# One layer's MLP recast in two phases, with its inner rows parked in DRAM and its second product done by seven block products

## The chip, the cores and the metric

The kernel runs on one core of a Trainium2 chip. A core has TensorE (PE in the profile, its weight load PEld), VectorE (DVE), ScalarE (ACT), GpSimd (POOL), and SyncE (SP), whose queue issues nearly all DMAs. TensorE writes to PSUM, which VectorE and ScalarE read; weights, activations and operands lie in SBUF. The metric is the device time of one execution in microseconds (us): the kernel before takes 1152.82 us, the median of three runs (1152.68 to 1153.12).

## The reference, cut to what matters

There are 512 latent and 256 context tokens (768 together) of width 1024, and two layers. Layer 0 mixes by pooling, layer 1 by attention, and each ends in a squared-ReLU MLP with inner width 4096. Before and after each part rows are normalised, scaled and shifted by vectors that come from a conditioning vector through `w_ada` (six slabs of 1024 columns a layer: shift, scale and gate for the mixer, then for the MLP).

```python
def sq_relu_mlp(h, w_in, w_out):
    return jnp.square(jax.nn.relu(h @ w_in)) @ w_out

# layer 0, latent and context tokens alike
m = sq_relu_mlp(modulate(rms_norm(x, g_mlp_pre), sh2, sc2), w_mlp_in, w_mlp_out)
x = x + gt2 * rms_norm(m, g_mlp_post)
```

Everything is float32. The kernel splits each operand into a high part in TensorE's rounded 32-bit type and a low part, the rest, and forms a product as three: high by high, high by low, low by high.

## The kernel before, in words

The change lies in the MLP of layer 0 (`mlp0`). Its inner width of 4096 is cut into 16 groups of 256 (`NG`), two blocks of 128 rows each. A group has two products. The first, `h @ w_in`, gives the group's inner rows (256 by 768 tokens). Groups 0 and 1 do it plainly (`Inner`). Groups 2 to 15 do it by a Strassen-Winograd scheme with seven block products (`Seven`): the 1024 of the contraction are halved, so are the tokens and the 256 inner rows, and seven products of half blocks, 12 matmuls of 384 columns each (`chain`), stand for eight. The sums of activation blocks are made once (`sums`), those of the weight blocks for every group (`weights_sums`): VectorE makes them, ScalarE rounds the high parts, VectorE subtracts for the low parts. Within a group the chains share four accumulators `a`, `b`, `c` and `e` in PSUM: chain 2 adds to `a` behind ScalarE's copy of `a` to `b`, chain 4 behind a copy of `a` to `c`, and chain 6 behind VectorE's reading of `a`.

ScalarE then takes ReLU and square, high and low parts go to SBUF (`hids0`), and the second product, `out_mm`, multiplies them by the group's 256 rows of `w_mlp_out`: for each of six tiles of 128 tokens and each half of 512 output columns 6 matmuls of 512 columns, 72 in a group. The result of each is added to `acc` in SBUF, mostly by VectorE (`out_ev`), in part by seeding the PSUM bank from `acc` through ScalarE and copying it back. The last two groups are done tile by tile in `finish`, where the normalisation that follows the MLP, and layer 1's query, key and value projections, run alongside.

Each group also works at the conditioning slabs that are needed later (`ada_step` in `mid0` and `extra0`): VectorE forms them in `ada_sum`, column by column of the contraction, for three slabs with both conditioning vectors (`dual`) and three with one (`lone`), and four small matmuls in `ada_fin` lay a slab down. In the stage before the MLP other slabs are formed by TensorE instead: `ada_mm` runs four float32 matmuls of a 128 by 32 stationary block on 512 columns for one loaded unit, each on its own 32 columns of the array, `ada_turn` transposes the result on VectorE, and `ada_sel` sums the pieces with small matmuls.

Raw weights pass through a pool of three buffers of 1 MB (`rawp`); SP issues the loads in order, and a load waits until its buffer is free. `work` tiles (`tmp`) come from a pool of three too. PSUM has two double tiles (`psA`, four banks) and four single ones (`psB`). The order on the engines is made by a planner that simulates the program with its own costs, within the dependences; in the stage before the MLP the code gives times by hand (`st.at`). The residual rows `xr` are parked in DRAM (`spill`) before the sums take their place in SBUF, and come back in `before0`.

## Time and profile before

| What | Value |
|---|---|
| median of three runs | 1152.82 us |
| profiled execution, first to last instruction (span) | 1150.8 us |
| what lies around the span, against the median | 2.0 us |
| PE, PEld busy | 1129.7 us (98%), 976.6 us (85%) |
| DVE, ACT, POOL busy | 925.9 us (80%), 640.0 us (56%), 76.0 us (7%) |
| traffic to and from DRAM | 154.20 MB, mean 134 GB/s |
| layer-0 MLP on TensorE, from group 1 to the end of the second product | 95.4 to about 586 us |

The profile holds one execution. A line of the groups gives engine and operation, the tiles written and read, shapes and count, then busy time, the mean of one instruction, and the idle time before them with what ended it. Nearly all instructions carry one line number, L68, since a helper records them; they are told apart by tiles: `psin` is the first product, `pso` the second, `psada` a conditioning slab on TensorE, `rows` one on VectorE, `units` and `rb` hold split weights and inner rows, `raw` a loaded weight, `acc` the running output. Matmul records overlap, so the time that one matmul really takes is read from start to start and not from its duration.

### The profile page before, as it was taken

How to read it: one execution, taken by the hardware profiler on the slowest of the kernel's cores; microseconds unless marked ns; L12 is line 12 of the kernel's file. 1: busy time of each engine (PE TensorE's matmuls, PEld its weight loads, DVE VectorE, ACT ScalarE, POOL GpSimd, SP SyncE). 2: the span in 40 equal slices, each digit the busy share in tenths (PEclk: the TensorE clock that was granted, in tenths of full speed). 3: DMA queues.
4: the chain of work that ended last, by engine and by line, in shares of the span. 5: the costliest groups of instructions: out<-in, count | busy, mean ns of one | idle time of the engine just before them, and what ended most of it. 6: DMA issues, size and time to landing. Idle time of an engine off the chain costs nothing. (4 is left out here: it accounts for less than half of the span.)

```text
span 1150.8 us, 15601 instructions
## 1 busy us (share of the span) xinstructions
PE 1129.7 (98%) x5998; PEld 976.6 (85%) x5998; DVE 925.9 (80%) x1539; ACT 640.0 (56%) x1142; POOL 76.0 (7%) x82
## 2 busy tenths in 40 slices
PE   6999999999999999999999999999999999999998
PEld 5579889998899988999878889988988888888886
DVE  5798488889889898897578688977887779778875
ACT  6476655554345434555795368863876436435534
POOL 3040000000000000000241312100000000000000
PEclk9999999999999999999999999999999999999999
DMA  9993233244434434344642200046244224224304
GB/s 352 399 391 105 74 110 110 80 140 147 144 113 147 146 130 146 128 143 145 227 145 104 98 1 19 17 144 225 75 146 147 78 69 146 81 66 147 110 17 149
DMA packets 100042, 154.20 MB, mean 134 GB/s; under 512 B 7120, under 2 KB 72448, under 8 KB 99968
## 3 DMA queue, kind: packets, MB, share of 16 engines
q1 hardware_dynamic: 99872, 153.19, 39.2%
q8 instruction: 47, 0.77, 0.3%
q14 instruction: 27, 0.22, 0.1%
q10 hardware_dynamic: 96, 0.02, 0.0%
HBM read 143.75 MB, written 9.45 MB: 133 GB/s over the span
## 5 line engine op out<-in xcount | busy, mean ns | idle before, releaser
L68 PE MATMUL pso<-units,rb 128*128 128x512 f32 x1152 | 277.7, 392 | 0.0
L68 PEld LDWEIGHTS pso<-units,rb 128*128 128x128 f32 x1152 | 214.8, 188 | 41.4
L68 DVE TENSOR_TENSOR acc<-acc,pso 128x512 f32<-128x512 f32 x192 | 128.3, 683 | 63.7 <-PE pso L68 63.6
L68 DVE SCALAR_TENSOR_TENSOR rows<-raw,cond,rows 128x256 f32<-128x256 f32 x280 | 122.2, 482 | 0.9
L68 PE MATMUL psin<-ra 128*128 128x512 f32 (+1 forms) x424 | 112.3, 369 | 0.6 <-ACT work L68 0.6
L68 PE MATMUL psin<-ra,rb 128*128 128x512 f32 (+1 forms) x384 | 101.6, 360 | 0.1
L68 DVE TENSOR_TENSOR units<-raw,units 128x1024 fp32r<-128x1024 f32 (+2 forms) x69 | 83.1, 1214 | 15.9 <-ACT units L68 15.8
L68 ACT CAST units<-raw 128x1024 fp32r<-128x1024 f32 (+2 forms) x71 | 70.8, 1019 | 41.6 <-PE pso L68 20.8
L68 PE MATMUL psin<-rb,ra 128*128 128x384 f32 (+1 forms) x324 | 90.6, 356 | 0.0
L68 PEld LDWEIGHTS psin<-ra 128*128 128x128 f32 x424 | 77.8, 188 | 12.1 <-ACT work L68 1.0
L68 PE MATMUL psin<-ra,units 128*128 128x384 f32 x432 | 82.5, 336 | 0.0
L68 PE MATMUL pso<-units,pairs 128*128 128x512 f32 x336 | 82.3, 389 | 0.0
L68 ACT ACTIVATE work<-psin 128x512 f32<-128x512 f32 (+3 forms) x66 | 36.1, 552 | 82.8 <-PE psin L68 75.1
L68 PEld LDWEIGHTS psin<-ra,units 128*128 128x128 f32 x432 | 76.5, 188 | 2.8
L68 PEld LDWEIGHTS psin<-ra,rb 128*128 128x128 f32 x384 | 66.7, 189 | 11.7 <-issue 0.9
L68 PEld LDWEIGHTS pso<-units,pairs 128*128 128x128 f32 x336 | 63.1, 188 | 13.1
L68 PE MATMUL psin<-sums,units 128*128 128x384 f32 x336 | 63.8, 336 | 0.0
L68 PEld LDWEIGHTS psin<-rb,ra 128*128 128x128 f32 x324 | 58.6, 188 | 5.4
L68 ACT COPY acc<-pso 128x512 f32<-128x512 f32 x68 | 38.6, 592 | 40.3 <-PE pso L68 40.2
L68 PEld LDWEIGHTS psin<-sums,units 128*128 128x128 f32 x336 | 59.1, 188 | 1.3
L68 ACT ACTIVATE work<-work 128x768 f32<-128x768 f32 (+1 forms) x50 | 41.4, 831 | 32.2 <-DVE work L68 31.7
L68 ACT CAST rb<-raw 128x2048 fp32r<-128x2048 f32 (+2 forms) x18 | 25.8, 1432 | 59.2 <-PE pso L68 55.9
(221 smaller groups left out, 2096.6 us busy)
## 6 DMA issues: line engine op xcount, KB each, us to landing
raw<-in_w_ada SPq DMA_DIRECT2D x48, 1024.0 KB, 5.4
raw<-in_w_mlp_in SPq DMA_DIRECT2D x32, 1024.0 KB, 5.3
raw<-in_w_mlp_out SPq DMA_DIRECT2D x32, 1024.0 KB, 5.7
raw<-in_w_qkv SPq DMA_DIRECT2D x6, 1024.0 KB, 5.1
spill<-xl SPq DMA_DIRECT2D x8, 512.0 KB, 10.8
xl<-spill SPq DMA_DIRECT2D x8, 512.0 KB, 10.9
raw<-in_w_o SPq DMA_DIRECT2D x4, 1024.0 KB, 5.0
xl<-in_x SPq DMA_DIRECT2D x4, 512.0 KB, 5.7
```

The costliest lines, as they stand in the source:

```text
L68: z = made(*args, **kw)
```

## The change

Layer 0's MLP is done in two phases. In the first, all groups form their inner rows; the squared rows go to a DRAM buffer `hidden` (float32, 32 blocks of 128 by 768) by SP's queue, and no second product stands between the groups. The split weights of successive groups alternate between two homes, and their accumulators between `psA` and `psB`. In the second phase the inner rows come back. Groups 0 to 11, as three stretches of 1024 of the contraction, are multiplied with `w_mlp_out` by seven block products each: tokens, contraction and output columns are halved, `prep` makes the sums and splits of a product two products ahead, `product_tile` runs 12 matmuls of 512 columns for each of three token tiles, and the results gather in seven blocks `M`, which `joins` combines in the third stretch. Groups 12 and 13 follow as plain products (24 matmuls for each of six tiles), and groups 14 and 15 in `finish` as before.

The three `dual` slabs move from VectorE to TensorE (`ada_dot`, `ada_end`): each is two halves of two units, set behind chain 3 and chain 5 of even groups 4 to 10, and within groups 1 and 2. The three `lone` slabs stay on VectorE. The residual rows are parked in DRAM earlier (`row_away`). The core of the diff:

```diff
+    def after(z, a):
+        if a is not None:
+            tc.add_manual_dep(z.ins, a.ins.name, ISSUE, reason="row order")
...
+    def ada_mm(i, m, c0, width, u, behind=None):
...
-                pin(te.matmul(ps[q:q + 32, :], cond[:, k, :], raw[:, kk, 512 * h:512 * h + 512],
-                              start=(u == 0), stop=(k >= KT - nk), skip_group_check=True), m in (GT1, SC2, SH2))
+                z = te.matmul(ps[q:q + 32, :], cond[:, k, :], raw[:, kk, 512 * h:512 * h + 512],
+                              start=(u == 0), stop=(k >= KT - nk), skip_group_check=True)
+                pin(z, m in (GT1, SC2, SH2))
+                after(z, behind)
...
+        if zeroed:
+            ve.memset(ps[:, 0:2 * n], 0.0)
...
+            if self.hid is None:
+                sy.dma_start(hidden[:, 2 * self.g + f], r)
+                return
...
-        B11, B21 = put(unit[1][:, 0:2048], rv[:, 0], 1024)
+        home = unit[2 - g % 2]
+        B11, B21 = put(home[:, 0:2048], rv[:, 0], 1024)
...
+            if g % 2 == 0:
+                hi, lo = (z.rearrange("p (m k n) -> p m k n", m=3, n=P)[:, m0:m0 + nm] for z in (rb[:, 0:1536], rb[:, 1536:3072]))
+            else:
...
+        def run(self, between=None, turns={}):
+            g = self.g
+            if g % 2:
+                a, e, b, c = (psB.tile([P, 512], F32, tag="b", name="psin")[:, 0:HN] for _ in range(4))
+            else:
+                px, py = (psA.tile([P, 2, 512], F32, tag="a", name="psin") for _ in range(2))
+                a, b, c, e = px[:, 0, 0:HN], px[:, 1, 0:HN], py[:, 0, 0:HN], py[:, 1, 0:HN]
+            if g == NG - 1:
+                r0, r1 = (work_tile()[:, 0:TOK] for _ in range(2))
+            else:
+                r0, r1 = (acc[:, TOK * z:TOK * z + TOK] for z in (2 * (g % 2), 2 * (g % 2) + 1))
+            if g == 3:
+                for z in (b, c):
+                    te.matmul(z, self.products[0][0][0][0], A11[0][0], start=True, stop=True)
...
+            if 3 in turns:
+                turns[3](self.ends[3])
...
+            if 5 in turns:
+                turns[5](self.ends[5])
...
-            hi, lo = self.hid
-            for f, r in enumerate((r0, r1)):
+            for f, r in ((1, r1), (0, r0)):
                 sc.activation(r, r, AF.Square)
-                sc.copy(hi[:, f, :], r)
-                ve.tensor_tensor(out=lo[:, f, :], in0=r, in1=hi[:, f, :], op=ALU.subtract)
+                sy.dma_start(hidden[:, 2 * g + f], r)
...
+    def row_away(t):
+        tc.keep_in_program_order(sy.dma_start(spill[:, t], xr[:, t]))
+
+    for t in (1, 2, 0, 3, 4, 5):
+        st.at(75.3 if t < 5 else 79.2, row_away, t)
...
-        wo_ = w_out(0, 0, one(unit[2]), True)
+        products = weights_sums(2)
+        halves = list(dual)
+        for u in range(2):
+            ada_load(*halves[0], 512, u)
         sums()
-        for g in range(NG - 1):
-            if g:
-                wo_, products = w_out(0, g, one(unit[2])), weights_sums(g + 1)
-            part = (g, inner.hid, wo_)
+        pinned[0] = False
+        inner = Inner(1, wi, aH, aL, None, chunks0, TOK)
+        inner.part(0, 0)
+        ada_dot(*halves[0], inner.last)
+        inner.part(0, 1, range(4))
+        ada_end(*halves[0], inner.last)
+        inner.part(0, 1, range(4, KT))
+        ada_dot(*halves[1], inner.last)
+        for f in range(2):
+            inner.square(f)
+        late_ = ExitStack()
+        NC = 3
+        W = [rb[:, 0:4096], unit[0], unit[1]]
+        regions = [(0, 0), (1, 0), (1, 1), (0, 1)]
+        xat = [n % 4 for n in range(7 * NC)]
+        xat[-3:] = [3, 0, 2]
...
+        def put(hi, lo, src):
+            sc.copy(hi, src)
+            ve.tensor_tensor(out=lo, in0=src, in1=hi, op=ALU.subtract)
...
+        def prep(n):
+            c_, z = divmod(n, 7)
+            a = lambda i, j: A[c_, i, j]
+            b = lambda j, h: B[c_, j, h]
...
+            if z == 0:
+                x, w = a(0, 0), b(0, 0)
+            elif z == 1:
+                x = done[c_, "s3"] = op(a(0, 0), a(0, 0), a(1, 0), ALU.subtract)
+                w = done[c_, "t3"] = op(t0, b(1, 1), b(0, 1), ALU.subtract)
+            elif z == 2:
+                x = op(X[1], a(1, 0), a(1, 1), ALU.add)
+                w = op(b(0, 1), b(0, 1), b(0, 0), ALU.subtract)
+            elif z == 3:
+                x = op(X[0], a(1, 1), done[c_, "s3"], ALU.subtract)
+                w = op(t0, done[c_, "t3"], b(0, 0), ALU.add)
+            elif z == 4:
+                x, w = op(X[0], a(0, 1), X[0], ALU.subtract), b(1, 1)
+            elif z == 5:
+                x, w = a(0, 1), b(1, 0)
+            else:
+                x, w = a(1, 1), op(t0, t0, b(1, 0), ALU.subtract)
+            u, h = regions[xat[n]]
+            hi, lo = (q[:, 4 * u:4 * u + 4, HN * h:HN * h + HN] for q in (hH, hL))
+            put(hi, lo, k3(x, HN))
+            wr = W[n % 3]
+            put(wr[:, 0:2048], wr[:, 2048:4096], w)
+            xs[n] = [[q[:, k] for k in range(4)] for q in (hi, lo)]
+            ws[n] = [[q[:, 512 * k:512 * k + 512] for k in range(4)] for q in (wr[:, 0:2048], wr[:, 2048:4096])]
+            if z == 2:
+                hid_load((c_, 0, 1), X[1])
+            elif z == 3:
+                row_load((c_, 1, 0))
+                rows_load(4 * NC) if end else row_load((c_ + 1, 0, 0))
+            elif z == 4:
+                pair_load(4 * NC, X[0]) if end else hid_load((c_ + 1, 0, 0), X[0])
+                rows_load(4 * NC + 1) if end else row_load((c_ + 1, 0, 1))
+            elif z == 5:
+                pair_load(4 * NC + 1, X[1]) if end else hid_load((c_ + 1, 1, 0), X[1])
+            elif z == 6:
+                pair_load(4 * NC + 2, X[2]) if end else hid_load((c_ + 1, 1, 1), X[2])
...
+        xs, ws = {}, {}
+        for g in range(2, NG):
+            now = products
+            if g < NG - 1:
+                products = weights_sums(g + 1)
+            else:
+                hid_load((0, 0, 0), acc[:, 3072:4608])
+                hid_load((0, 1, 0), acc[:, 4608:6144])
+                for key in ((0, 0, 0), (0, 0, 1), (0, 1, 1)):
+                    row_load(key)
             extra(g)
-            if g:
-                inner = Seven(products, hids[(g + 1) % len(hids)])
+            seven = Seven(now, g)
+            turns = {}
+            if g == 2:
+                turns[3] = lambda z: ada_end(*halves[1], z)
+            elif g % 2 == 0 and g <= 10:
+                half = halves[g // 2]
+                for u in range(2):
+                    ada_load(*half, 512, u)
+                turns[3] = lambda z: ada_dot(*half, z)
+                turns[5] = lambda z: ada_end(*half, z)
+            seven.run(lambda: mid(g), turns)
...
+        prep(0)
+        prep(1)
+        S["held"].close()
+        top.close()
+        pool = late_.enter_context(tc.tile_pool(name="late", bufs=1, side="right"))
+        for z in range(3):
+            X[z] = pool.tile([P, 4 * HN], F32, name=f"x{z}")
+        X["t"] = pool.tile([P, 2048], F32, name="t0")
+        low = pool.tile([P, 512], F32, name="m1")
+        Mp = top.enter_context(tc.tile_pool(name="sevens", bufs=1)).tile([P, 8, 512], F32, name="m")
+        hid_load((0, 1, 1), X[2])
...
+        tiles = [(n, t) for n in range(7 * NC) for t in tts]
+        by_add = lambda n, t: n % 2 == 1 and t == tts[1] or n % 7 == 6 and t == tts[2]
+        banks = {}
+
+        def open_bank(q):
+            if q >= len(tiles):
+                return
+            n, t = tiles[q]
+            banks[q] = psB.tile([P, 512], F32, tag="b", name="pso")
+            if n >= 7 and not by_add(n, t):
+                sc.copy(banks[q], M[n % 7][t])
+
+        def product_tile(q):
+            n, t = tiles[q]
+            ps, d = banks.pop(q), M[n % 7][t]
+            seed = n >= 7 and not by_add(n, t)
+            (aH, aL), (wH, wL) = xs[n], ws[n]
+            for k in range(4):
+                for m, (a, w) in enumerate(((aH, wH), (aH, wL), (aL, wH))):
+                    te.matmul(ps, a[k][:, P * t:P * t + P], w[k], start=(k == 0 and m == 0 and not seed),
+                              stop=(k == 3 and m == 2), skip_group_check=seed)
+            if n < 7 or seed:
+                sc.copy(d, ps)
             else:
-                inner = Inner(g + 1, wi, aH, aL, hids[(g + 1) % len(hids)], chunks0, TOK)
-            inner.run((lambda: mid(g)) if g < NG - 2 else None)
-            if g == NG - 2:
-                wo_ = w_out(0, NG - 1, one(unit[1]))
-            else:
-                for t in range(NT):
-                    out_mm(0, [part], t)
-                    out_ev(0, [part], t)
+                ve.tensor_tensor(out=d, in0=d, in1=ps, op=ALU.add)
...
+        open_bank(0)
+        open_bank(1)
+        for q, (n, t) in enumerate(tiles):
+            if t == tts[0] and n + 2 < 7 * NC:
+                prep(n + 2)
+            if (n, t) == (7 * NC - 1, tts[0]):
+                put2(hid_a[0], A[4 * NC])
+                put2(w_a[0], B[4 * NC])
+                put2(hid_a[1], A[4 * NC + 1])
+                rows_load(4 * NC + 3)
+                pair_load(4 * NC + 3, X[0])
+            open_bank(q + 2)
+            product_tile(q)
+            if n >= 7 * NC - 7:
+                joins(n % 7, t)
+        put2(w_a[1], B[4 * NC + 1])
+        put2(hid_b[0], A[4 * NC + 2])
+        put2(hid_b[1], A[4 * NC + 3])
+        late_.close()
+        top.close()
+        open_top()
...
         before_last()
+        put2(wo_[0], B[4 * NC + 2])
+        put2(wo_[1], B[4 * NC + 3])
+        pairs = [(h, w) for h, w in zip(hid_a, w_a)]
+        for t in order:
+            ts_ = slice(place_of[t] * P, (place_of[t] + 1) * P)
+            seed = t not in order[0:2]
...
+            seq = [(a, f, w) for (hi, lo), (wH, wL) in pairs for f in range(2) for a, w in ((hi, wH), (hi, wL), (lo, wH))]
+            line = sorted(((n, h) for n in range(len(seq)) for h in range(2)), key=lambda z: (z[0] >= 9, z[1]))
+            for n, h in line:
+                a, f, w = seq[n]
+                te.matmul(pss[h], a[:, f, ts_], w[:, f, 512 * h:512 * h + 512], start=(n == 0 and not seed),
+                          stop=(n == len(seq) - 1), skip_group_check=seed)
+            for h in range(2):
+                d = accv[:, t, 512 * h:512 * h + 512]
+                if seed:
+                    sc.copy(d, pss[h])
+                else:
+                    ve.tensor_tensor(out=d, in0=d, in1=pss[h], op=ALU.add)
         order0.extend(order)
-        behind_chains.extend(inner.ends[z] for z in (4, 6))
-        finish(0, [part, (NG - 1, inner.hid, wo_)], order, last)
-        del behind_chains[:]
+        finish(0, [(4 * NC + 2 + z, hid_b[z], wo_[z]) for z in range(2)], order, last)
...
-    dual = [(0, GT2, 2), (1, SC1, 2), (1, SH1, 2)]
-    lone = [(1, m, 1) for m in (GT1, SC2, SH2)]
...
-        for u in [u for u in due if u[0] <= 0]:
-            ada_fin(*u[1:])
...
+    dual = [(i, m, c0) for i, m in ((0, GT2), (1, SC1), (1, SH1)) for c0 in (0, 512)]
+    lone = [(1, m) for m in (GT1, SC2, SH2)]
+
+    def ada_dot(i, m, c0, z):
+        for u in range(2):
+            ada_mm(i, m, c0, 512, u, z)
+        ada_turn(i, m, c0)
+        ve.memset(adaps[i, m, c0][:, 0:8], 0.0)
+
+    def ada_end(i, m, c0, z):
+        ada_sel(i, m, c0, 512, z)
+        ada_add(i, m, c0, 512)
 
     def mid0(g):
-        if g > 1:
-            ada_step()
+        n, j = divmod(g - 2, 4)
+        if 0 <= n < len(lone):
+            at = 32 * n + 8 * j
+            ada_sum(*lone[n], j, 1, parts[0][:, at:at + 8])
```

More of the change, by code (lines that the diff above doesn't have):

```diff
@@ L134, in backbone, with open_top @@
     unit, pinned = [rb[:, 6144:10240]], [True]
+    top = ExitStack()
+    def open_top():
+        unit[2:] = [top.enter_context(tc.tile_pool(name="top", bufs=1)).tile([P, 4096], F32R, name="units")]
     def open_units():
@@ L138, in open_units @@
         pools[0] = rawp
-        units = ctx.enter_context(tc.tile_pool(name="units", bufs=1)).tile([P, 2 * 4096], F32R, name="units")
-        unit.extend(units[:, 4096 * i: 4096 * (i + 1)] for i in range(2))
+        unit.append(ctx.enter_context(tc.tile_pool(name="units", bufs=1)).tile([P, 4096], F32R, name="units"))
+        ctx.callback(top.close)
+        open_top()
     hH = ra[:, 0:KT * TOK].rearrange("p (k n) -> p k n", n=TOK)
@@ L738, in part @@
                             s_ = a[:, k].rearrange("p (h m) -> p h m", h=2)[:, :, t0:t0 + ln]
-                        pin(te.matmul(d, w[:, k, fs], s_,
-                                      start=(k == 0 and n == 0), stop=(k == KT - 1 and n == self.final)), on)
+                        self.last = te.matmul(d, w[:, k, fs], s_,
+                                              start=(k == 0 and n == 0), stop=(k == KT - 1 and n == self.final))
+                        pin(self.last, on)
         def busy(self, c, n):
@@ L1027, in backbone @@
     pso = {}
-    order0, behind_chains = [], []
+    order0 = []
     def out_mm(i, parts, t, cols=HALVES):
@@ L1066, in out_ev @@
             d = accv[:, t, c0:c0 + w]
-            if parts[0][0] == 0:
-                sc.copy(d, ps)
-            elif seeded[t]:
-                sc.copy(d, ps)
-            else:
-                ve.tensor_tensor(out=d, in0=d, in1=ps[:, 0:w], op=ALU.add)
+            ve.tensor_tensor(out=d, in0=d, in1=ps[:, 0:w], op=ALU.add)
     def finish(i, parts, order, last, also=()):
@@ new lines, in joins @@
+        def joins(z, t):
+            add = lambda d, a, b, f=ALU.add: ve.tensor_tensor(out=d[t], in0=a[t], in1=b[t], op=f)
+            if z == 3:
+                add(M6, M6, M1)
+                add(M7, M7, M6)
+            elif z == 4:
+                add(M3, M3, M6)
+                add(M3, M3, M5)
+            elif z == 5:
+                add(M2, M2, M1)
+            elif z == 6:
+                add(M4, M7, M4, ALU.subtract)
+                add(M7, M7, M5)
+        two = lambda z, n: (k3(z[:, 0:n], n // 2), k3(z[:, n:2 * n], n // 2))
@@ new lines, in mlp0, with put2 @@
+        hid_a = [two(ra[:, 0:3072], 1536), two(ra[:, 6144:9216], 1536)]
+        w_a = [two(unit[0], 2048), (k3(ra[:, 3072:5120], D), k3(ra[:, 9216:11264], D))]
+        hid_b = [two(z, 1536) for z in (rb[:, 0:3072], rb[:, 3072:6144])]
+        def put2(hl, src):
+            (hi, lo), src = hl, k3(src, hl[0].shape[-1])
+            for f in range(2):
+                put(hi[:, f], lo[:, f], src[:, f])
+        open_bank(0)
[13 more added lines that the diff above has]
+                joins(n % 7, t)
```

138 lines of the change are left out of this document (70 added, 68 removed).

## The prediction

> **What bounds the kernel now.** I read the page's head and engine shares first, then the stretches of the MLP.
>
> ```profile
> span 1150.8 us, 15601 instructions
> PE 1129.7 (98%) x5998; PEld 976.6 (85%) x5998; DVE 925.9 (80%) x1539; ACT 640.0 (56%) x1142; POOL 76.0 (7%) x82
> ...
> 143.00:174.00 31.00, 31.00 (x156) 28.00 (x156) 24.10 (x41) 17.27 (x27) 0.00 (x0) 1.00 0.31 102
> 267.00:298.00 31.00, 31.00 (x162) 27.68 (x162) 27.95 (x55) 14.93 (x22) 0.00 (x0) 1.00 0.44 143
> ```
>
> A stretch gives its length, then busy time of PE, PEld, DVE, ACT and POOL, the granted clock (1.00), the DMA share and GB/s. These two are one group each, and TensorE never stops in them. Durations overlap, so I test that by start times, in TensorE's timeline:
>
> ```profile
> 190.97 2.27 PE L68 MATMUL psin<-ra,units 128*128 128x384 f32 x12
> 193.07 2.24 PE L68 MATMUL psin<-sums,units 128*128 128x384 f32 x12
> ...
> 553.12 22.19 PE L68 MATMUL pso<-units,rb 128*128 128x512 f32 x97
> 575.15 0.38 PE L68 MATMUL psx<-ident,acc 128*128 128x128 f32 x2
> ```
>
> A chain of the first product takes 193.07 - 190.97 = 2.10 us, 0.175 us a matmul; a matmul of the second takes (575.15 - 553.12) / 97 = 0.227 us. A group is 84 x 0.175 + 72 x 0.227 = 31.0 us, the whole stretch. So the MLP costs what its matmuls cost, and a matmul taken out is worth its pitch, if nothing new stops the stream. VectorE has 27.95 of 31 us filled (90%) and still stops nothing: TensorE's own waits from 100 to 560 us are these three rows (total us, times, longest).
>
> ```profile
> PEld psada L68 <- issue: 1.5, 5, 0.4
> PEld psada L68 <- DVE units L68: 0.2, 1, 0.2
> PEld psin L68 <- DVE work L68: 0.2, 1, 0.2
> ```
>
> **The change on TensorE.** The first product keeps its matmuls. The second has 1152 of 512 columns now, the count of this row:
>
> ```profile
> L68 PE MATMUL pso<-units,rb 128*128 128x512 f32 x1152 | 277.7, 392 | 0.0
> ```
>
> After the change it is 3 stretches x 7 products x 3 tiles x 12 = 756, 144 for groups 12 and 13 and 144 in the last stage, 1044 together. 108 fewer, at 0.227: **-24.5 us**.
>
> The slabs come on top: three slabs of two halves of two units, 12 units of four matmuls, and six small sums.
>
> ```profile
> 58.56 1.92 PE L68 MATMUL psada<-raw,cond 128*32 128x512 f32 x16
> 60.42 6.02 PE L68 MATMUL pspool<-rb,ra 128*128 128x256 f32 x48
> 66.37 3.64 PE L68 MATMUL psada<-raw,cond 128*32 128x512 f32 x32
> 69.82 0.33 PE L68 MATMUL psada<-work,mods 128*32 128x8 f32 x16
> ...
> 71.10 0.25 PE L68 MATMUL psada<-work,sel 128*32 128x8 f32 x8
> 71.28 0.98 PE L68 MATMUL psx<-ident,acc 128*128 128x128 f32 x7
> ...
> 287.14 0.26 PE L68 MATMUL psada<-parts,sel 128*32 128x16 f32 x8
> 287.34 4.08 PE L68 MATMUL psin<-sums,units 128*128 128x384 f32 x22
> ```
>
> A matmul of a unit leaves two records. Sixteen records, two units, take 60.42 - 58.56 = 1.86 us; four units take 3.45, or 0.86 each. The change runs them in pairs: 6 x 1.86 = **+11.2 us**. A sum takes 71.28 - 71.10 = 0.18 us, six **+1.1 us**. The three small steps of these slabs that fall away take 287.34 - 287.14 = 0.2 us each, **-0.6 us**, and two added matmuls in group 3 cost 2 x 0.175 = **+0.35 us**. TensorE's sum is -24.5 + 11.2 + 1.1 - 0.6 + 0.35 = **-12.4 us**.
>
> **What the other engines must do, and when.** Their durations:
>
> ```profile
> L68 DVE SCALAR_TENSOR_TENSOR rows<-raw,cond,rows 128x256 f32<-128x256 f32 x252 | 109.1, 482 | 0.3
> L68 DVE TENSOR_TENSOR acc<-acc,pso 128x512 f32<-128x512 f32 x116 | 76.8, 682 | 29.8 <-PE pso L68 29.7
> L68 DVE TENSOR_TENSOR units<-raw,units 128x1024 fp32r<-128x1024 f32 x46 | 56.1, 1221 | 14.0 <-ACT units L68 13.8
> L68 ACT CAST units<-raw 128x1024 fp32r<-128x1024 f32 x46 | 47.7, 1049 | 31.9 <-PE pso L68 13.1 <-DMA raw<-in_w_mlp_in 12.7 <-PE psin L68 6.1
> L68 DVE TENSOR_TENSOR rb<-work,rb 128x768 fp32r<-128x768 f32 x34 | 32.4, 954 | 7.0 <-ACT rb L68 6.9
> L68 ACT COPY acc<-pso 128x512 f32<-128x512 f32 x56 | 31.7, 592 | 40.0 <-PE pso L68 39.9
> L68 DVE TENSOR_TENSOR work<-raw 128x512 f32<-128x512 f32 x28 | 19.2, 687 | 6.2 <-DMA raw<-in_w_mlp_in 6.1
> L68 DVE TENSOR_TENSOR work<-work,psin 128x384 f32<-128x384 f32 x28 | 15.5, 553 | 13.2 <-PE psin L68 12.9
> L68 ACT COPY psin<-psin 128x384 f32<-128x384 f32 x28 | 13.1, 468 | 25.8 <-PE psin L68 25.8
> ```
>
> *First phase.* A group on TensorE is 14.7 us, 16.7 with a half slab. VectorE's part: weight sums and splits 3 x 1.221 + 5 x 0.687 = 7.1, two adds 1.1, one piece of a lone slab, eight products at 0.482 at most and some 0.85 for transpose and reduction (estimated from the 256-column row with these widths), 4.7; a half slab adds 0.7 (priced as a 512-column operation). That is 12.9 of 14.7 us (88%) in odd groups and 13.6 of 16.7 in even ones, less than the 90% borne now. The slabs' former VectorE work and the splits of inner rows leave at no gain, off the path.
>
> What does change is the cover. Three times in a group a chain waits for a reader of `a`, with just one chain of 2.10 us between; today blocks of the second product also stand there. ScalarE's copy with one cast ahead of it takes 0.468 + 1.049 = 1.52 us, VectorE's add with one split ahead 0.553 + 1.221 = 1.77: both fit. With two ahead they take 2.57 and 3.00, late by 0.47 and 0.90. Bounds for 14 groups: 0, and 14 x (0.47 + 0.47 + 0.90) = 25.8 us. The next group has accumulators and weight homes of its own, so its chains can move up; I take 1.5 us, near the end that the waits row shows. What stands behind a chain that waits is all of TensorE's queue.
>
> A half slab's units wait on two loads, in a three-buffer pool that holds a unit until TensorE has read it.
>
> ```profile
> raw<-in_w_ada SPq DMA_DIRECT2D x48, 1024.0 KB, 5.4
> raw<-in_w_mlp_in SPq DMA_DIRECT2D x32, 1024.0 KB, 5.3
> raw<-in_w_mlp_out SPq DMA_DIRECT2D x32, 1024.0 KB, 5.7
> spill<-xl SPq DMA_DIRECT2D x8, 512.0 KB, 10.8
> ```
>
> ```profile
> GB/s 352 399 391 105 74 110 110 80 140 147 144 113 147 146 130 146 128 143 145 227 145 104 98 1 19 17 144 225 75 146 147 78 69 146 81 66 147 110 17 149
> ```
>
> Two groups (31 us) load six buffers, so each buffer has 15 us for a load of 5.4 and its reader: no stall. In the same 31 us 6.3 MB are loaded and 1.6 MB of inner rows stored, 250 GB/s against 399 at the page's peak, so I cost bandwidth at nothing. A store waits on SP for the square and holds later loads for some 3 us; a group's weights are fetched a group ahead, which hides it.
>
> *Start.* Group 1 no longer has a second product of 16.3 us behind it while the sums are made.
>
> ```profile
> 95.44 16.81 PE L68 MATMUL psin<-ra,units 128*128 128x384 f32 x96
> ...
> 118.32 0.96 DVE L68 TENSOR_TENSOR sums<-work,sums 128x768 fp32r<-128x768 f32 x1 [2.16 <-ACT sums L68]
> ```
>
> With two half slabs group 2 starts at 95.4 + 16.8 + 3.9 = 116.1. VectorE now ends the sums at 119.3, having also split inner rows and weights of `w_mlp_out` meanwhile (about 8 us), which fall away; the residual rows leave earlier on SP, so nothing new holds the sums' place. Chains 4 and 5 need the last sums, at 116.1 + 8.4 = 124.5. Bounds 0 and 3; I take 0.5.
>
> *Handover.* Products 0 and 1 need `prep`: splits of 1536 and 2048 columns and, for most, two sums of these widths. By the slope of the rows (0.687 at 512, 1.221 at 1024) a 1536-column operation is an estimated 1.76 us and a 2048-column one 2.29, so a `prep` with both sums is 8.1 us of VectorE. TensorE's product is 36 x 0.227 = 8.2. Preps 1, 2 and 3 in a row each cost 8.1; prep 1's weight home comes free only with chain 5 of group 15, and prep 2 also waits for an operand loaded into the place of the sums. Behind the end of group 15 VectorE has some 8 us left of prep 1 against a cover of 8.2, and prep 2 is due at 16.3. Bounds: 0, and 6 us if the five loads start only behind group 14's stores. I take 1.
>
> *Seven products.* A stretch of the contraction is 57.2 us of TensorE. VectorE: 7 x 4.05 for the splits, 4 x 1.76 + 4 x 2.29 for the sums, 4.5 adds at 0.683: 47.6 us (83%). ScalarE: at 1.049 for 1024 columns some 24 us of casts and 33 bank copies of 0.59 in later stretches, 43 us. Both run two products ahead. The third stretch has 21 joins (14.3 us) and the splits of groups 12 and 13 (6.3) but only five preps: 56 of 57. At the 90% that VectorE fills today it would be 62, so bounds 0 and 5; joins may run on into the 33 us behind, so 0.5.
>
> *Last two steps.* Half of group 13's weights can be split only behind product 20, 1.05 + 1.22 us, against six matmuls (1.4 us) of cover. Bounds 0 and 2.5, taken 0.5. The residual rows (10.8 us a load) have group 12 and 13's 33 us to come back: nothing.
>
> New stops 1.5 + 0.5 + 1 + 0.5 + 0.5 = 4 us, so -12.4 + 4 = **-8.4 us**. The span would be 1142.4; with the 2.0 us around it, which I keep, **1144.4 us** against 1152.8.
>
> **The rivals.** *All covered.* No new stop: 1152.8 - 12.4 = 1140.4. For it speaks that VectorE at 90% stops nothing today; against it, that the blocks of the second product that filled every gap are gone.
>
> *The handover and the third stretch bind.* VectorE becomes the bound there: 6 + 5 us at the upper bounds, 2.5 elsewhere, so 1152.8 - 12.4 + 13.5 = 1153.9; at half of the 11 us 1148.4. For it: 56 of 57 us and three preps of 8.1 against 8.2. Against: it must miss at both places.
>
> *The chains stall on their own accumulators (the other side).* In the first phase a chain waits for `a` behind two queued operations at each of the three places, 25.8 us at the bound above, so 1152.8 - 12.4 + 25.8 + 2.5 = 1168.7; at half of it 1156. It decides from (12.4 - 2.5) / 14 = 0.7 us a group. For it: ScalarE's copies and VectorE's adds stand in queues that are 57 and 88% full. Against: two sets of accumulators and homes let the next group fill in.
>
> ```profile
> L68 PE MATMUL psada<-raw,cond x160: 592/592/618, 16.3 to 77.0; 128*32 128x512 f32 x160
> ```
>
> *The slab matmuls run one behind the other.* A record lasts 0.592 us in this row; 96 in single file are 57 us, so 1152.8 - 12.4 + 4 + 45.6 = 1190. Against it, 16 records take 1.86 us in the timeline above, since the four stand in different columns of the array.
>
> The Trainium skill, FP8 and Floating Point Precision (TensorE Precision Notes), says that true float32 makes four passes through the array. At the 2.4 GHz that the Trainium skill's TensorE: Matmul & The Clock Gate (Part 1) gives, 48 matmuls of 512 columns in single file would be an estimated 42 us, and the sum by it some 22 us slower than before. Part 3 of that page of the Trainium skill has 32-column blocks run side by side, which would make it 10 us; with that the trace agrees, 1.86 us for two units.
>
> **How the numbers follow.** Forecast 1144.4 with its own range of 1141 to 1149: 0.55. All covered: 0.14. Handover and third stretch: 0.12, of which half lies within 0.2% (2.3 us, about what a measurement can tell from no change). Chains: 0.18, mostly slower. Slab matmuls in single file: 0.01. Faster 0.55 + 0.14 + 0.03 = 0.72, the same 0.06 + 0.02 = 0.08, slower 0.20. The low end is below all covered by a microsecond or so for pitches read a little high, 1139; the high end reaches into the chains' rival at half its price, 1156.
>
> **What would show it.** Matmuls of the second product: 1044. A group of the first phase 14.7 us, 16.7 with a half slab; a longer one, with TensorE idle behind ScalarE's `psin` copies or VectorE's add, speaks for the chains. Products of 8.2 us from the second on; TensorE idle behind VectorE at the first three or in the third stretch speaks for the handover. VectorE busy falls by over 50 us without worth. The last stage and layer 1 should keep their length; if they don't, I have missed a step.

## The result and the profile after

The changed kernel takes **1178.05 us** (median; 1177.68 to 1178.36) against 1152.97 (1152.68 to 1153.38) beside it: ratio 1.0216, 95% interval 1.0201 to 1.0230. The forecast was 1144.4 with a range of 1139 to 1156, so it was wrong in sign: 25 us slower, not 8 faster. The profiled execution's span is 1176.4 us, 25.6 above that of before.

The head of the page after, then stretches of the layer-0 MLP, columns as in the prediction:

```profile
span 1176.4 us, 15518 instructions
...
PE 1127.7 (96%) x6012; PEld 963.3 (82%) x6012; DVE 882.5 (75%) x1270; ACT 668.2 (57%) x1139; POOL 74.9 (6%) x82
```

```profile
95.67:133.00 37.33, 26.35 (x148) 21.37 (x149) 24.22 (x38) 17.64 (x24) 0.00 (x0) 0.82 0.77 257
133.00:160.00 27.00, 27.00 (x169) 26.57 (x168) 12.53 (x20) 9.02 (x14) 0.00 (x0) 1.00 0.58 132
160.00:176.00 16.00, 10.45 (x45) 9.94 (x44) 13.08 (x23) 10.93 (x16) 0.00 (x0) 0.79 0.49 160
176.00:243.00 67.00, 64.22 (x392) 58.57 (x390) 46.15 (x88) 32.15 (x48) 0.00 (x0) 1.00 0.68 224
243.00:361.00 118.00, 115.17 (x687) 109.03 (x688) 84.32 (x149) 57.83 (x84) 0.00 (x0) 1.00 0.64 216
361.00:390.00 29.00, 22.96 (x88) 18.02 (x88) 27.17 (x15) 15.29 (x16) 0.00 (x0) 0.82 0.48 166
390.00:545.00 155.00, 155.00 (x685) 128.35 (x684) 121.11 (x83) 106.37 (x125) 0.00 (x0) 1.00 0.40 130
545.00:612.80 67.80, 67.18 (x304) 55.45 (x303) 36.67 (x46) 39.57 (x81) 11.35 (x10) 1.00 0.46 162
```

Before, TensorE filled 490.60 of the 490.66 us of this part. Now it stands still 11.0 us at the start, 5.6 from 160 to 176, 2.8 and 2.8 in the rest of the first phase and 6.0 at the handover: 28 us, and the three worst stretches are just those with a granted clock of about 0.8. The second phase is as the prediction had it.

TensorE's timeline with the waits in these stretches (start, length, then the idle time before and what ended it):

```profile
115.18 1.06 PE L68 MATMUL psada<-raw,cond 128*32 128x512 f32 x8 [0.48 <-DMA raw<-in_w_ada]
118.39 1.07 PE L68 MATMUL psada<-raw,cond 128*32 128x512 f32 x8 [2.15 <-DMA raw<-in_w_ada]
122.49 1.01 PE L68 MATMUL psin<-ra,units 128*128 128x384 f32 x2 [3.03 <-ACT units L68]
128.82 4.21 PE L68 MATMUL psin<-ra,units 128*128 128x384 f32 x12 [5.32 <-ACT work L68]
...
165.13 4.21 PE L68 MATMUL psin<-ra 128*128 128x384 f32 x12 [4.94 <-DVE acc L68]
...
372.95 0.96 PE L68 MATMUL pso<-rb,ra 128*128 128x512 f32 x3 [1.27 <-ACT rb L68]
375.97 0.79 PE L68 MATMUL pso<-units,ra 128*128 128x512 f32 x1 [2.05 <-ACT units L68]
379.48 10.65 PE L68 MATMUL pso<-rb,ra 128*128 128x512 f32 x33 [2.72 <-DVE rb L68]
```

The twelve matmuls behind a wait of about 5 us take 4.21 us instead of 2.1, and 33 of 512 columns take 10.65 instead of 33 x 0.227 = 7.5. Each long wait is paid again in clock. In the expectations below, the "loss" of a stretch holds both: its length less each matmul in the timeline times its pitch (some records are missing from a trace, which reads as loss, so it is good to a few microseconds). In the changed kernel it is 14.1 us at the start, 8.0 from 160 to 175, 4.1 and 3.5 up to 361, 9.9 at the handover, about 0 behind. Together that is 39.6 us; with -12.4 for TensorE's matmuls it makes 27.2 us, against 26.7 us by which layer 1 begins later (612.83 against 586.09 us). Layer 1 itself is 1.1 us shorter.

What is late, read from SP's timeline (issue times) and, behind it, from one row of ScalarE and two of VectorE:

```profile
80.20 0.39 SPq L154 DMA_DIRECT2D raw<-in_w_mlp_in  x1
97.29 1.05 SPq L786 DMA_DIRECT2D hidden<-work  x2
98.44 0.41 SPq L154 DMA_DIRECT2D raw<-in_w_mlp_in  x1
98.94 12.89 SPq L154 DMA_DIRECT2D raw<-in_w_ada  x4
...
146.57 0.98 SPq L408 DMA_DIRECT2D grows<-gc  x2
149.64 0.37 SPq L154 DMA_DIRECT2D raw<-in_w_mlp_in  x1
```

```profile
162.92 1.05 ACT L68 CAST units<-raw 128x1024 fp32r<-128x1024 f32 x1 [11.92 <-DMA raw<-in_w_mlp_in]
162.92 1.29 DVE L68 TENSOR_TENSOR work<-raw 128x512 f32<-128x512 f32 x2 [8.57 <-DMA raw<-in_w_mlp_in]
...
164.53 0.55 DVE L68 TENSOR_TENSOR acc<-acc,psin 128x384 f32<-128x384 f32 x1
```

At the start SP waits from 80.6 to 97.3 for group 0's squares, which it is to store, and group 2's weights and the slab's stand behind that store. At 146.57 the two stores of layer 0's gate columns go out, and the weight load behind them lands 13.3 us after its issue, where 5.4 is usual. ScalarE waits for it 11.92 us, with the finished group's last steps queued behind. VectorE waits 8.57 us for it, and the add at 164.53 that stands behind in its queue is the one that ends TensorE's wait at 165.13. The DMA view from 145 to 165 us:

```profile
DMA packets 3162, 1.10 MB, mean 55 GB/s; under 512 B 2105, under 2 KB 3161, under 8 KB 3161
...
raw<-in_w_mlp_in SPq DMA_DIRECT2D x1, 1024.0 KB, 13.3
grows<-gc SPq DMA_DIRECT2D x2, 4.0 KB, 12.3
```

The gate stores are 2 x 1024 pieces of four bytes. The kernel before has them too, but at 292.26, with the next weight load issued 12 us later. There a load of `w_mlp_out`, issued 0.4 us ahead of them, took 12.5 us as well, and TensorE didn't stop for it:

```profile
291.84 0.37 SPq L147 DMA_DIRECT2D raw<-in_w_mlp_out  x1
292.26 2.55 SPq L391 DMA_DIRECT2D grows<-gc  x2
304.06 0.37 SPq L147 DMA_DIRECT2D raw<-in_w_mlp_in  x1
...
raw<-in_w_mlp_out SPq DMA_DIRECT2D x1, 1024.0 KB, 12.5
```

At the handover, VectorE's timeline:

```profile
367.20 2.28 DVE L68 TENSOR_TENSOR acc<-raw 128x2048 f32<-128x2048 f32 x1
...
371.07 2.28 DVE L68 TENSOR_TENSOR raw<-raw 128x2048 f32<-128x2048 f32 x1
373.27 2.29 DVE L68 TENSOR_TENSOR t<-acc,raw 128x2048 f32<-128x2048 f32 x1
...
377.14 2.29 DVE L68 TENSOR_TENSOR rb<-acc,rb 128x2048 fp32r<-128x2048 f32 x1
```

Prep 1's weight sum is written into `acc[:, 0:2048]`, where group 14's rows lie until they are stored; it comes at 367.20, behind sums of prep 2. No wait for the store itself shows in VectorE's rows, so why the planner put the sum so late isn't shown; experiment 2 tests the place. VectorE then does the sums of preps 2 and 3 ahead of the split of prep 1 (377.14), for which TensorE stands.

### The profile page after: what moved, and what is told of

It is laid out like the page before. It is cut to its first block, busy times and chain, and to the rows that moved or that the text cites. A ratio compares the mean times of both kernels' runs of the same rounds, so it can differ in the third digit from the quotient of the medians.

```text
span 1176.4 us, 15518 instructions
## 1 busy us (share of the span) xinstructions
PE 1127.7 (96%) x6012; PEld 963.3 (82%) x6012; DVE 882.5 (75%) x1270; ACT 668.2 (57%) x1139; POOL 74.9 (6%) x82
## 5 line engine op out<-in xcount | busy, mean ns | idle before, releaser
L68 PE MATMUL pso<-rb,ra 128*128 128x512 f32 x576 | 137.8, 396 | 4.6 <-DVE rb L68 2.7
L68 PEld LDWEIGHTS pso<-rb,ra 128*128 128x128 f32 x576 | 109.9, 191 | 29.0 <-DVE rb L68 3.2
L68 PE MATMUL psin<-ra,rb 128*128 128x512 f32 (+2 forms) x468 | 118.1, 357 | 0.5 <-DVE acc L68 0.4
L68 DVE TENSOR_TENSOR acc<-acc,pso 128x512 f32<-128x512 f32 x90 | 60.7, 684 | 60.8 <-PE pso L68 60.8
L68 ACT CAST units<-raw 128x1024 fp32r<-128x1024 f32 (+2 forms) x47 | 49.4, 1079 | 61.7 <-DMA raw<-in_w_mlp_in 45.6
L68 DVE TENSOR_TENSOR rb<-raw,rb 128x2048 fp32r<-128x2048 f32 (+2 forms) x41 | 62.1, 1514 | 15.8 <-ACT rb L68 15.6
L68 PE MATMUL psin<-rb 128*128 128x512 f32 (+2 forms) x242 | 73.7, 356 | 0.0
L68 PE MATMUL psin<-rb,ra 128*128 128x512 f32 (+1 forms) x226 | 70.2, 365 | 0.0
L68 DVE TENSOR_TENSOR work<-raw 128x512 f32<-128x512 f32 (+1 forms) x42 | 35.3, 865 | 40.8 <-DMA raw<-in_w_mlp_in 40.8
L68 PE MATMUL pso<-units,ra 128*128 128x512 f32 x252 | 59.5, 391 | 2.1 <-ACT units L68 2.1
L68 PEld LDWEIGHTS pso<-units,ra 128*128 128x128 f32 x252 | 47.4, 188 | 12.3 <-ACT units L68 2.5
## 6 DMA issues: line engine op xcount, KB each, us to landing
raw<-in_w_qkv SPq DMA_DIRECT2D x6, 1024.0 KB, 12.5
```

Of the source, the lines that this page charges most:

```text
L68: z = made(*args, **kw)
```

## The experiments

**1. Whose queue the store stands in.** The stores of the inner rows go out on ScalarE, which makes the squares, instead of on SP.

```
-                sy.dma_start(hidden[:, 2 * self.g + f], r)
+                sc.dma_start(hidden[:, 2 * self.g + f], r)
...
-                sy.dma_start(hidden[:, 2 * g + f], r)
+                sc.dma_start(hidden[:, 2 * g + f], r)
```

> The only edit: the stores of the inner rows are issued by ScalarE, right behind the square that makes them, instead of by SP. In the changed kernel (1178.1) TensorE lost some 14 us before group 2, 15 us more by group 6 and 10 us at the handover, against the sum of its matmuls. Theory Q, queue order: on SP a store that waits for a square stands ahead of the weight loads behind it (group 2's weights left at 98.4 us behind the store of group 0, where SP was free at 80.6). Then group 2's weights leave at about 81, the loss before group 2 falls from 14 to 6 or less and that of the groups from 15 to 6 or less: 1156 to 1165. Rival B, buffers: loads wait for one of three raw buffers whoever stores: within 3 us of 1178. Rival C, chains that wait for their own accumulators, as the prediction had it: within 3 us of 1178.

Measured 1171.93 us, ratio 1.0164 (1.0149 to 1.0179): 6.1 us back. Group 2's weights are issued at once, at 80.39, and TensorE's waits for `w_ada` at the start are gone. The cause is real but smaller than expected: the wait <-ACT work stays, 5.66 us at 122.81, and from 133 to 361 us TensorE still idles 11.5 us, where the changed kernel has 11.2.

**2. Where prep 1's weight sum lies.** It goes into two work tiles, and group 15's rows into `acc`.

```
-                w = done[c_, "t3"] = op(t0, b(1, 1), b(0, 1), ALU.subtract)
+                w = done[c_, "t3"] = [op(work_tile(), cut(b(1, 1), i), cut(b(0, 1), i), ALU.subtract) for i in range(2)]
...
-            if g == NG - 1:
-                r0, r1 = (work_tile()[:, 0:TOK] for _ in range(2))
```

> Prep 1's first weight sum goes to two work tiles instead of columns 0 to 2047 of acc, and group 15's rows to acc instead of work tiles; all else as in the changed kernel. Theory H: at the handover VectorE's sum for product 1 waited until 367.2 us for the store of group 14's rows to leave that place in acc, and the splits of product 1 came after the sums of preps 2 and 3; 10 us of TensorE went there. With its own place the sum runs at about 363 and 4 to 9 us come back: 1169 to 1174, with the first phase unchanged. Rival V: three preps of 8.1 us of VectorE against products of 8.2 set it, wherever the sum lies: within 3 us of 1178.

Measured 1171.2 us, ratio 1.016 (1.0139 to 1.018): 6.9 back, as expected. Prep 1's sum comes at 352.87 in place of 367.20. The handover's waits of 1.27, 2.05 and 2.72 us become 1.06 and 0.90, and the 33 matmuls run in 7.65 us instead of 10.65.

**3. Both.**

> Both edits, stores by ScalarE and a home of its own for prep 1's weight sum. By Q and H together the gains add, 13 to 22 and 4 to 9: 1147 to 1161. If one cause hides the other, it comes out at the better of the two alone. By B, C and V 1175 to 1181.

Measured 1164.13 us, ratio 1.0098 (1.0081 to 1.0114): 13.9 back, and 6.1 + 6.9 = 13.0. The gains add, though the time lies 3 us above the expected range; 11 us over the kernel before are left.

**4. The two phases without the slabs on TensorE.** The three slabs stay with VectorE, as before.

```
-        ada_dot(*halves[0], inner.last)
...
-                turns[3] = lambda z: ada_dot(*half, z)
-                turns[5] = lambda z: ada_end(*half, z)
...
+    dual = [(0, GT2, 2), (1, SC1, 2), (1, SH1, 2)]
```

> One part alone: the two phases without the slab matmuls; the three slabs stay on VectorE as in the kernel before. TensorE has 12 us less to do. By the rows VectorE then has 8.2 us a group for weights and adds and 163 us of slab work, 278 us against TensorE's 206 for 14 groups: the first phase, 266 us now, becomes some 300, and the time 1205 to 1225. Rival B: the slab units hold raw buffers until TensorE comes to them, which makes the loads late; without them loads come early and the time falls to 1150 to 1165.

Measured 1209.98 us, ratio 1.0496: 32 us slower than the whole change. First the stretch from 130 to 390 us here, then 130 to 360 of the changed kernel:

```profile
130.00:390.00 260.00, 221.14 (x1147) 204.48 (x1146) 227.92 (x481) 109.03 (x159) 0.00 (x0) 0.93 0.59 190
```

```profile
130.00:360.00 230.00, 218.85 (x1292) 205.68 (x1291) 155.09 (x277) 110.21 (x163) 0.00 (x0) 0.98 0.63 204
```

VectorE is filled 88% here against 67%, and TensorE idles 39 us. The slabs on TensorE are what makes the two phases affordable, and leaving their matmuls out doesn't bring the 25 us back. What their units cost by holding raw buffers can't be read here, since VectorE sets the pace; experiment 10 comes back to it.

**5. Whether the small elements block a queue or the transfer engines.** Experiment 3 still loses some 10 us around 160, where its weight load lands 14.9 us after its issue. The gate stores alone move to ScalarE's queue.

```
-            sy.dma_start(rows_out[row_of[i, m, ci]].rearrange("(k p) -> p k", p=P), gc)
+            (sc if (i, m) == (0, GT2) else sy).dma_start(rows_out[row_of[i, m, ci]].rearrange("(k p) -> p k", p=P), gc)
```

> The kernel of e3 with one edit: the two stores of layer 0's gate columns (gate_away, grows<-gc, 1024 elements of four bytes each) are issued by ScalarE instead of SP. In e3 they go out at 137.47 us, the weight load behind them on SP at 138.70 lands at 153.65, 15 us later, and TensorE idles 4.30 us at 158.41 and then runs 12 products in 4.21 instead of 2.25 us; from 129.6 to 175 e3 loses 10.3 us against its matmuls at full pitch. Theory S (the load stands behind the small elements in SP's own queue): it lands some 5 to 6 us after its issue, the wait at 158 goes, 5 to 9 us come back: 1155 to 1159 us. Rival C (the small elements hold the DMA engines, whichever engine issues them): the load lands as late as before, no gain: 1162 to 1166 us.

Measured 1163.15 us (1.0088, 1.0073 to 1.0103): no gain beyond the spread of experiment 3 (1161.84 to 1165.93). The DMA view from 138 to 158 us:

```profile
raw<-in_w_mlp_in SPq DMA_DIRECT2D x1, 1024.0 KB, 14.6
...
grows<-gc ACTq DMA_DIRECT2D x2, 4.0 KB, 12.7
```

Another queue, the same delay: theory S falls, and C is left. The Trainium skill, DMA: Bandwidth & Descriptors (Issuing engines are not separate DMA queues), says that transfers end on the same 16 engines and interleave whichever engine started them; the trace agrees, 14.6 us with two queues and 14.9 with one.

**6. Group 1 alone.** Its squares are made in `acc`, and its second half uses two single banks.

```
-            r = work_tile()[:, 0:self.ntok]
+            own = self.g == 1 and self.ntok == TOK
+            r = acc[:, TOK * (2 + f):TOK * (3 + f)] if own else work_tile()[:, 0:self.ntok]
...
+                if self.g == 1 and f == 1 and self.ntok == TOK:
+                    self.ps[z] = [psB.tile([P, 512], F32, tag="b", name="psin") for _ in range(2)]
```

> The kernel of e3 with group 1 changed alone: its squares are built in acc (free by then) instead of two of the three work tiles, which the stores hold, and its second half accumulates in two of the single banks (psB), so that group 2's first chain needs no bank of group 1; one dummy product more in group 2. e3 loses 7.4 us from 95.8 to 129.6 (5.41 us idle at 121.92 <-ACT work, then 12 products in 3.90 us). Theory R (group 2 waits for group 1's rectified tiles, late for want of a work tile): the wait goes, 4 to 7 us come back: 1157 to 1160 us. Rival V (ScalarE and VectorE are simply not done with the sums and splits of the start, group 2's operands come next): under 2 us, 1162 us or more.

Measured 1163.09 us (1.0091, 1.0076 to 1.0106): 1 us, where R had 4 to 7, and that is within the spread. Yet the start is mended, TensorE idling 1.4 us up to 130 us instead of 5.4. Group 4's chain behind ScalarE's first copy, in experiment 3 and then here, and a later wait here:

```profile
168.88 3.58 PE L68 MATMUL psin<-ra,units 128*128 128x384 f32 x12 [1.75 <-ACT psin L68]
```

```profile
165.11 2.38 PE L68 MATMUL psin<-ra,units 128*128 128x384 f32 x12 [0.55 <-ACT psin L68]
...
271.74 3.91 PE L68 MATMUL psin<-ra,units 128*128 128x384 f32 x12 [2.96 <-ACT psin L68]
```

At group 4 the 3.8 us are still there. They go later: from 180 to 280 us TensorE idles 7.8 us here against 3.5 in experiment 3, and at group 10 (271.74 against 270.61) the kernel is behind. Why these waits grow isn't shown. R was right about the place and wrong about the worth; the edit moves the squares and the banks at once, and the two aren't told apart.

**7. Five and six together.**

> The edits of e5 and e6 together on e3. If S and R hold and the two stalls are separate, the gains add: 9 to 16 us, 1148 to 1155 us, about the kernel before. If an earlier group 2 only meets the next late operand (rival L: the start is bound by its loads and splits), no more than the better of the two alone: 1156 to 1160 us.

Measured 1160.96 us (1.0072, 1.0051 to 1.0094). The sum of the single gains, about 2, would be 1162; no 9 to 16 came, since S had fallen. Its four runs spread from 1158.23 to 1164.64, so the 2 us are not told from nothing.

**8. The gate stores 150 us later.**

```
-        if g in (7, 8):
-            gate_away(0, GT2, g - 7)
+        if g in (11, 12):
+            gate_away(0, GT2, g - 11, S["end"])
```

> The kernel of e3 with the two gate stores kept on SP but made to wait for the last product of groups 10 and 11, so that they go out some 150 us later, each in front of one weight load. Theory S with position as the cause (at 137 us the weight ring has no reserve, later it has): the stall at 158 goes and none takes its place: 1155 to 1159 us, as e5. If any weight load behind them pays (the reserve is never there): the stall moves to two places near 270 to 300 us, 1160 to 1167 us. Under rival C as well the stall at 158 goes, so this run alone does not tell S from C; e5 does.

Measured 1167.38 us (1.013, 1.0112 to 1.0148): 3 us worse than experiment 3. The stall at 158 goes, TensorE being filled 48.89 of 50 us from 130 to 180, but the two loads behind the new places pay. From 280 to 325:

```profile
280.00:325.00 45.00, 37.62 (x192) 36.48 (x191) 25.43 (x44) 17.55 (x27) 0.00 (x0) 0.89 0.87 152
```

A load issued at 281.46 is used by ScalarE at 293.95, after a wait of 10.30 us. Both new places cost; the load at 281.46 has just one of the two stores beside it and takes 12.4 us to land. That leaves the form of the stores as the suspect.

**9. The gate columns turned first.** VectorE's block transposition puts 32 elements of a row in line, so the same 8 KB go out as 64 pieces of 128 bytes. It stands on experiment 6.

```
+        z, y = acc[:, 5120:5152], acc[:, 5152:5184]
...
+        ve.transpose(y, z)
+        for ci in range(2):
+            for b in range(4):
+                sy.dma_start(rows_out[ci].rearrange("(k b i) -> b k i", b=4, i=32)[b], y[32 * b + 8 * ci:32 * b + 8 * ci + 8, :])
```

> The kernel of e6 with layer 0's gate columns turned on VectorE by its 32x32 block transposition and written to their rows as eight stores of 8 x 32 elements (64 pieces of 128 bytes) in place of two stores of 1024 elements of four bytes each. e5 had the small elements on ScalarE's queue, and the weight load issued at 140.40 us still landed only at 154.99; so theory C is taken up: the small elements hold the DMA engines. If C holds, the weight load behind lands some 5 to 8 us after its issue as in e8 (139.12 to at most 146.6), the loss of 11.2 us that e6 has between 130 and 180 falls to about 2, as in e8, and no stall comes up at 290 to 320: 1152 to 1157 us. If it is the halves of w_ada and the reloads around that place that hold the engines (rival B): 1161 us or more, the load still lands 10 us or more after its issue.

Measured 1152.57 us, ratio 0.9997 (0.9988 to 1.0007): 10.5 us back by this edit alone, level with the kernel before. The weight load among these stores, from 130 to 145 us, and TensorE from 130 to 180, first here, then in experiment 6:

```profile
raw<-in_w_mlp_in SPq DMA_DIRECT2D x1, 1024.0 KB, 5.4
...
130.00:180.00 50.00, 49.04 (x291) 46.44 (x290) 37.07 (x68) 25.36 (x37) 0.00 (x0) 1.00 0.69 229
```

```profile
130.00:180.00 50.00, 41.49 (x232) 38.58 (x231) 28.20 (x51) 18.40 (x27) 0.00 (x0) 0.93 0.71 195
```

The load takes 5.4 us again, and 7.5 us of idle time and the low clock go. One reload of inner rows also moves behind, from 128.52 to 140.73 us, since the turned columns use its place; experiment 11 has no such reload here and small elements, and its load is late.

**10. A slot less taken from the inner weights.** From group 4 on, half of each half slab goes into the idle part of `acc`.

```
-                for u in range(2):
-                    ada_load(*half, 512, u)
+                loaded[(*half, 0)] = acc[:, 3072:5120].rearrange("p (k n) -> p k n", n=512)
...
+                sy.dma_start(loaded[(*half, 0)], w_ada[i_, 0:512, m_ * D + c_:m_ * D + c_ + 512].rearrange("(k p) n -> p k n", p=P))
+                ada_load(*half, 512, 1)
```

> e9 with one more edit: from group 4 on the first half-load of each slab unit goes into the part of acc that is idle in the first phase, instead of one of the three weight slots, so that the next inner weights need not wait for the slab's products to free theirs; the early reload of the inner rows into the same part then comes behind the last of these. Theory W (three slots for two streams: the waits of ScalarE and VectorE for w_mlp_in from 180 to 360 us, and through their queues TensorE's waits at 199, 235 and 271, come from the slot): the loss of e6 between 180 and 280 us (11.4 us) falls to 4 or less, 1146 to 1151 us, below the kernel before. Rival O (the waits there are ScalarE's queue order, a copy of psin behind another group's work, not the loads): within 2 us of e9.

Measured **1143.4 us** (1142.86 to 1144.2), ratio 0.9916 (0.9901 to 0.9931): 9.2 us below experiment 9, more than expected, and faster than both kernels. The edit also keeps the early reload of inner rows into that part of `acc` back to the end of the phase; the two effects aren't told apart. TensorE from 180 to 280, experiment 9 and then 10:

```profile
180.00:280.00 100.00, 93.37 (x562) 84.44 (x561) 69.07 (x129) 45.77 (x69) 0.00 (x0) 0.98 0.68 227
```

```profile
180.00:280.00 100.00, 98.18 (x607) 91.53 (x606) 74.75 (x139) 49.84 (x75) 0.00 (x0) 1.00 0.75 248
```

**11. Ten with the gate stores as they were.**

> e10 with the two stores of layer 0's gate columns put back as they were: 1024 elements of four bytes each, on SP, in front of a weight load. e9 gained 10.5 us over e6 by the turned gates alone while the weight ring had no reserve; e10 frees one slot of the ring, but this one weight load is issued at the same moment (134.0 us) in e9 and e10. If the small elements cost what they did because the load behind them cannot be issued earlier (theory C, the reserve does not reach it): about 10 us over e10, 1150 to 1155 us. If the reserve of the ring takes them up (rival): 1143 to 1147 us.

Measured 1152.98 us, ratio 1.0004 (0.9994 to 1.0014): 9.6 us over experiment 10. The freed slot doesn't take up the small elements; the load behind them takes 12.7 us. So the form of the stores decides, with the rest of the kernel alike.

**12. The changed kernel with the edits of 9 and 10 alone.**

> The changed kernel itself with the two edits on transfers alone (gates turned, first half-loads of the slabs in the idle part of acc); stores of the inner rows stay on SP, prep 1's sum stays in acc, group 1 stays as it was. If the causes are separate, it keeps the losses of the start (14.1 us less the 0.5 to 2 that e10 still has there) and of the handover (9.9 us), and gets back those from 160 to 361 us (15.6 us): 1160 to 1164 us. If the stores on SP also hold the loads of the middle, so that the reserve does nothing while they stand in the same queue (rival): 1166 us or more.

Measured 1167.83 us, ratio 1.013 (1.0115 to 1.0145): 10.2 back, where separate causes had 14 to 18. The number is in the rival's range. TensorE's waits of 2.52, 2.14 and 5.32 us at the start and 1.77, 2.06 and 2.32 at the handover are all there, as both readings have it. In the middle the edits work in part: from 160 to 361 us TensorE idles 5.1 us, against 11.2 in the changed kernel and 1.8 in experiment 10, and the second phase starts 9.6 us sooner (351.59 against 361.18). So of the 15.6 us some 10 come back and 5 stay. ScalarE's waits for inner weights show the same (total, times, longest):

```profile
ACT units L68 <- DMA raw<-in_w_mlp_in: 30.1, 7, 6.4
```

The changed kernel has 45.6 us there and experiment 10 has 10.8. The stores on SP, which experiment 10 has on ScalarE's queue, may hold these loads, as the rival says; the other edits differ too, and what keeps the 5 us isn't shown.

## Why the prediction was wrong

**TensorE's sum, -12.4 us: right.** The second product has 576 + 252 + 144 + 72 = 1044 matmuls:

```profile
L68 PE MATMUL pso<-rb,ra 128*128 128x512 f32 x576 | 137.8, 396 | 4.6 <-DVE rb L68 2.7 <-ACT rb L68 1.3 <-ACT pso L68 0.6
L68 PE MATMUL pso<-units,ra 128*128 128x512 f32 x252 | 59.5, 391 | 2.1 <-ACT units L68 2.1
L68 PE MATMUL pso<-units,rb 128*128 128x512 f32 x144 | 33.4, 391 | 0.0
L68 PE MATMUL pso<-ra 128*128 128x512 f32 x72 | 18.0, 389 | 0.0
```

The slab units run mostly alone (1.06 us for 8 records, as at 115.18) and not in pairs, so they cost about 12 to 13 us instead of 11.2. Experiment 10 has the same matmuls, but for two more of 0.175 us, and few stops, some 4.4 us of idle time in the MLP, and its layer 1 begins 8.8 us sooner than before (577.29 against 586.09): -12.4 with 4.4 us of stops gives -8.0. Layer 1 is 1.0 us shorter there, which makes the 9.8 us under before.

**The start, 0.5 us with bounds 0 and 3: failed, 14.1.** I looked at VectorE and the sums and not at what SP has ahead of group 2's loads. The sentence that fails is "A store waits on SP for the square and holds later loads for some 3 us; a group's weights are fetched a group ahead, which hides it." At the start the store waits 16.7 us (80.6 to 97.3) and no group is ahead. The other part, group 1's banks and the work tiles that its stores hold, I hadn't seen at all; it stood as 5.32 us of idle time and the low clock, and experiment 6 takes that wait away.

**Bandwidth, costed at nothing: failed.** 250 of 399 GB/s was the wrong measure. The delay comes from 8 KB in four-byte pieces that went out at 292 us before and go out at 147 now, since their slab is done early. The prediction lists the slab's loads and small steps and not these two stores. It is worth 9.6 (experiment 11 against 10) to 10.5 us (9 against 6).

**Three buffers, "15 us for a load of 5.4 and its reader: no stall": failed.** ScalarE's waits for inner weights in the first phase (total, times, longest), in after and then in experiment 10:

```profile
ACT units L68 <- DMA raw<-in_w_mlp_in: 45.6, 13, 11.9
```

```profile
ACT units L68 <- DMA raw<-in_w_mlp_in: 10.8, 4, 3.9
```

While ScalarE waits, its queue brings copies and rectified tiles late. Experiment 10 is 9.2 us better than 9 with the slot freed, not told apart from the reload held back. The step that failed is the 15 us taken as enough: it has no term for a load that stands behind others in SP's queue, nor for a slot held until TensorE comes to its unit. Which of them weighs more stays open.

**The handover, 1 us with bounds 0 and 6: failed in size, 9.9.** I had loads behind group 14's stores for the upper bound; it was the place of prep 1's weight sum, in `acc` over rows to be stored (6.9 us by experiment 2). The upper bound lacked the clock.

**The clock** has no term in the prediction. By the 4.21 against 2.1 us twice and the 10.65 against 7.5, about 7 us of the 25 are the slower matmuls behind long waits. The Trainium skill, TensorE: Matmul & The Clock Gate (Part 1), says the clock halves after an idle window of about 3.4 us and comes back after as long a busy one. The trace agrees for the waits of about 5 us, which are followed by some 4 us at half pace; but in experiment 11 a wait of 2.09 us, shorter than that window, was followed by twelve matmuls in 3.58 us, so a shorter wait can cost clock too.

**The chains on their own accumulators, 1.5 us:** their sign came true, and it misleads. Of the 11.2 us that TensorE idles from 133 to 361 us, 4.6 stand in three waits for ScalarE's `psin` copies and 5.3 in two for VectorE's adds. What held the readers up, in the wait of 4.94 us at 165.13, was a load ahead of them in their queue (162.92), not two casts or splits as the rival had it. With the transfers mended, experiment 10 keeps five such waits, 2.8 us together, so the rival, priced at 1168.7 us, falls, though its sign alone couldn't show that.

**What held:** the seven products run at full pitch (155.00 of 155 us filled), the last two steps have one wait of 0.62 us, layer 1 keeps its length (563.6 us from the first of its matmuls to the end, 564.7 before). VectorE falls by 43.4 us, not over 50, and "at no gain" holds only beside the kernel before: experiment 4 shows 32 us for it inside the change.

A group of the first phase was to take 14.7 us, 16.7 with a half slab, 31.4 for two. Experiment 10, same chain of every second group:

```profile
188.15 2.37 PE L68 MATMUL psin<-ra,units 128*128 128x384 f32 x12 [0.61 <-ACT psin L68]
220.65 2.37 PE L68 MATMUL psin<-ra,units 128*128 128x384 f32 x12 [0.61 <-ACT psin L68]
```

32.5 us, of which 0.6 is the wait.

## What to carry to other kernels

When a change moves a step, list every transfer it issues, tiny ones too, with what stands behind each in its new place: here 8 KB decided 10 us. A store that waits for its data belongs on the queue of the engine that makes the data, not on the one that fetches what comes next (6.1 us here). And when a mended stall gives nothing, look where the time went before giving up the theory: experiment 6 was worth 1 us at the end, though its 3.8 us still stood at group 4, and waits behind took them.

## What the runs showed of the hardware

Stores of 1024 four-byte elements delay a 1 MB load beside them from 5.4 us to 12.4 to 15.4 (in ten of these kernels, at 131 to 147, 278 and 292 us, on two queues, and 12.4 with one such store alone), whereas the same bytes in 64 pieces of 128 don't (5.4 us in experiments 9, 10 and 12). And waits of about 5 us were followed by twelve matmuls in 4.21 us in place of 2.1, in stretches with a granted clock of 0.79 to 0.82.
